# Rotary key beside the latents, norms by two blocks, and new rooms for attention's loads in a two-layer hybrid decoder

## The chip, the cores and the metric

The kernel runs on one core of a Trainium2 chip. Its time is device microseconds of one execution, as the median over runs. Engines are named as in the profile: PE (TensorE), DVE (VectorE), ACT (ScalarE), POOL (GpSimd), SP (SyncE); PEld is PE's weight load. DMA transfers are issued from the queues of SP, ACT and POOL.

## The reference

Two decoder layers of one sequence of 1024 tokens and width 1024, all in f32. In each layer:

```
h = x @ w_in                                  # split by columns into
  hg_q, hg_f, hg_i, hg_gate                   # HGRN2, 8 heads of 128: gated linear recurrence
  mla_cq (256), mla_ckv (128), mla_kr (32)    # latent attention, 8 heads
  mla_gate (512), mem_q, mem_gate             # attention into 256 memory tokens, 4 heads
q = rmsnorm(cq) @ w_uq -> 8 x (64 nope + 32 rope);  q_rope = rope(...)
c = rmsnorm(ckv);  k_nope = c @ w_uk;  v = c @ w_uv
k_rope = rope(kr)                             # one rotary key, shared by all heads
p = softmax(causal((q_nope k_nope + q_rope k_rope) / sqrt(96)));  y_mla = p v
y = concat(y_hg silu(hg_gate), y_mla silu(mla_gate), y_mem silu(mem_gate)) @ w_out
x = layernorm(4**0.25 * x + y)
```

## The kernel before

All products are made with f32 values split in two parts, a high one ("h", rounded) and a low one ("l", the rest): three matmuls for one (`mm3`, high x high, high x low, low x high). A split is an ACT cast and a DVE difference (`split`, L289 and L290; `slab_aps`, L248 and L249, for weight slabs).

A layer has five stages. (1) `mem_attn`: projections of the memory heads and attention into the memory. (2) `latents_out`: cq, ckv and kr for two halves q of the tokens, four blocks of 128 tokens each. `latents` accumulates the four blocks of a half in PSUM, over four k of the first weight slab and then over four of the second. `norm` then takes the squares of all four blocks on ACT, a power on POOL (L858) and the scaling on ACT and DVE. Once both halves are through, `turn` transposes the normalised latents on PE, scales and splits them and stores them to DRAM (CQ, CK). The raw rotary key is kept in SBUF (`kr`). `spread` loads x again, in pieces "t", and makes from the blocks of x the operands T1 to T4 of the next stage. (3) `hgrn_group`: every slab of 256 columns is projected by seven half-size products (B11, T1, T2, B22, T3, B21, T4 in this order) instead of eight, with sums before (`diff`) and after (`put`). It runs over four pairs of heads, and the last pair is followed by two slabs of gates for attention (`mla_gates`), which go through tiles "G" to DRAM (MG). (4) `mla_prep` and `mla_attend`: weights w_uv, w_uk (`kv`) and w_uq (`uq`) are loaded and split, ckT and cqT loaded back, the rotary key is made (`rope_key`, six DVE operations, three copies, eight transposes, eight splits of 64 rows into K), then keys (`k_proj`, `k_odd`), queries (`q_proj`), values (`v_proj`), scores, softmax and values. (5) `out_group`: output projection and layer norm.

The order of the instructions on every engine is written by a planner before the program runs: it takes them by their order in the code, but lets a later one go ahead if the earlier is not ready by its estimates. On the chip each engine works through its own list in order and waits at semaphores. Tiles with one tag share a fixed number of rooms (the last argument of `T`), handed out in the order in which they became free. Pools follow each other in the same bytes of SBUF, and the first write to a tile of a later pool waits until every earlier tile that overlaps any byte of it has had its last reader, a DMA store included. The rooms that matter, as byte ranges of a partition: HGRN's F 28672 to 40960 and Q 40960 to 53248, three of 4096 each; G 88384 to 96576, two; attention's weight slabs "wh" from 24576 and "wl" from 40960, two of 8192 each; the key's tile "kb" 86016 to 90112; X, the operands of the products, 163328 to 228864 (X[i][j], block row i, token half j, 16384 each); T2, T3, T4 114176 to 163328; ckT, cqT and rtab 57344 to 86016; the t pieces 82176 to 102656, over the memory values (81920 to 90112). In PSUM, HGRN's "Y" lies on the banks of the tag that the stage before took first: "A" in layer 0, "B" in layer 1.

Of the kernel before, what the change touches and what calls it, by code (L numbers as in the profile page):

```python
# [81 lines left out]
def program(tc, xT, xtok, memT, pos, w_in, small, w_uq, w_uk, w_uv, w_mk, w_mv,  # L82
# [185 lines left out]
    def xs(X, i, kc, th):  # L268
        return X[kc // 4][th][i][:, kc % 4]
# [26 lines left out]

    CQ = [[T(dr, [2, P, S], F32, f"CQd{l}{i}") for i in range(2)] for l in range(DEPTH)]
    CK = [[T(dr, [P, S], F32, f"CKd{l}{i}") for i in range(2)] for l in range(DEPTH)]
    MG = [T(dr, [4, P, S], F32, f"MGd{l}") for l in range(DEPTH)]


# [340 lines left out]
    def spread(l, X, hp, lp):  # L642

        B11, B12, B21, B22 = X[0][0], X[0][1], X[1][0], X[1][1]
        T2, T3, T4 = ([T(hp, [P, 4, 512], F32R, f"t{n}{h}", 1) for h in range(2)] for n in (2, 3, 4))

        def piece():
            return T(lp, [P, 512], F32, "t", 10)

        src = xT if l == 0 else XT1  # L650
        for k in range(4):
            raw = {}
            for i, j in ((0, 0), (0, 1), (1, 1), (1, 0)):
                raw[i, j] = piece()
                nc.scalar.dma_start(raw[i, j], src[(4 * i + k) * P:(4 * i + k + 1) * P, j * 512:(j + 1) * 512])
            t1, t2, t3, t4 = raw[0, 1], raw[1, 1], piece(), raw[1, 0]
            nc.vector.tensor_tensor(out=t3, in0=t2, in1=t1, op=ALU.subtract)
            nc.vector.tensor_tensor(out=t1, in0=t1, in1=raw[0, 0], op=ALU.subtract)
            nc.vector.tensor_tensor(out=t2, in0=t2, in1=t1, op=ALU.subtract)
            nc.vector.tensor_tensor(out=t4, in0=t4, in1=t2, op=ALU.subtract)  # L660
            for o, t in ((B12, t1), (T2, t2), (T3, t3), (T4, t4)):
                split(o[0][:, k], o[1][:, k], t)
        return dict(B11=B11, T1=B12, T2=T2, B22=B22, T3=T3, B21=B21, T4=T4)

    def hgrn_group(l, X):

        with ExitStack() as gs_:
# [93 lines left out]
                return G  # L761

            def mla_gates(i2):
                G = [T(sp, [P, S], F32, "G", 2) for _ in range(2)]
                slab_w(O_MG + 256 * i2, silu_put(G, lambda i, j, g: nc.gpsimd.dma_start(
                    MG[l][2 * i2 + i, :, j * 512:(j + 1) * 512], g)))

# [54 lines left out]
    def latents_out(l, X, tp):  # L822

        with pool(f"c{l}", bufs=1, reuse_waits="tile") as lp:
# [9 lines left out]
            def latents(q, w):  # L834
                if q == 1:
                    accs = [a[:, 512 * i:512 * i + NC] for a in (psA(), psA()) for i in range(2)]
                else:
                    accs = [psB()[:, 0:NC] for _ in range(4)]
                for half in range(2):
                    for b in range(4):  # L840
                        s_ = slice(b * P, (b + 1) * P)
                        for k in range(4):
                            kc = 4 * half + k
                            mm3(accs[b], xs(X, 0, kc, q)[:, s_], xs(X, 1, kc, q)[:, s_], w[half][0][:, k], w[half][1][:, k],
                                kc == 0, kc == KC - 1)
                return accs

            def norm(q, accs):
                cq, ck = (T(lp, [P, 4, 256], F32, "pr", 4) for _ in range(2))
                ss = T(lp, [P, 2, 4], F32, "ss", 4)  # L850
                for b in range(4):
                    for i, (c, c0, c1) in enumerate(((cq, 0, 256), (ck, 256, 384))):
                        nc.scalar.activation(c[:, b, 0:c1 - c0], accs[b][:, c0:c1], AF.Square, accum_out=ss[:, i, b:b + 1])
# [4 lines left out]
                nc.gpsimd.tensor_tensor(out=r, in0=ss.rearrange("p a b -> p (a b)"), in1=mhalf, op=ALU.pow)  # L858
                for b in range(4):
                    nc.scalar.activation(ck[:, b, 0:128], accs[b][:, 256:384], AF.Copy, scale=r[:, 4 + b:5 + b])  # L860
                    nc.vector.tensor_scalar(out=cq[:, b], in0=accs[b][:, 0:256], scalar1=r[:, b:b + 1], scalar2=None,
                                            op0=ALU.mult)
                    nc.vector.tensor_copy(kr[:, 4 * q + b], accs[b][:, 384:NC])
                return cq, ck

            def turn(si, q, cn):
                s_ = slice(q * 512, (q + 1) * 512)
                for rc in range(2 - si):
                    pt = psB()
                    for b in range(4):  # L870
                        nc.tensor.transpose(pt[:, b * P:(b + 1) * P], cn[:, b, rc * P:(rc + 1) * P], ident)
                    g = sm[:, 18 + 2 * l + rc:19 + 2 * l + rc] if si == 0 else sm[:, 22 + l:23 + l]
                    h, lo = (T(lp, [P, 512], F32R, f"c{x}", 2) for x in "hl")
                    nc.scalar.activation(h, pt, AF.Copy, scale=g)
                    nc.vector.scalar_tensor_tensor(out=lo, in0=pt, scalar=g, in1=f32(h), op0=ALU.mult, op1=ALU.subtract)
                    for i, t in enumerate((h, lo)):
                        nc.sync.dma_start(CQ[l][i][rc, :, s_] if si == 0 else CK[l][i][:, s_], f32(t))

            w = [slab_c(0), slab_c(1)]
            c1 = norm(1, latents(1, w))  # L880
            c0 = norm(0, latents(0, w))
            for q, c in ((1, c1), (0, c0)):
                for si in range(2):
                    turn(si, q, c[si])
            return spread(l, X, tp, lp)

    def mla_prep(l, lp, rp):

# [3 lines left out]
        rtab = T(lp, [P, S], F32, "rtab", 1)  # L892

        def ld_kv(raw):
            nc.sync.dma_start(raw[:, 0:512], w_uv[l])
# [33 lines left out]
        def rope_key():  # L929

            k4 = T(lp, [P, NB, P], F32, "kb", 1)
            tmp = T(lp, [P, 512], F32, "qf", 2)[:, 0:NB * RD].rearrange("p (b r) -> p b r", b=NB)
            for hv in range(2):
                a, b = (cosk, sink) if hv == 0 else (sink, cosk)
                o_ = k4[:, :, 16 * hv:16 * hv + 16]
                nc.vector.tensor_tensor(out=o_, in0=kr[:, :, 0:16], in1=a, op=ALU.mult)
                nc.vector.tensor_tensor(out=tmp, in0=kr[:, :, 16:32], in1=b, op=ALU.mult)
                nc.vector.tensor_tensor(out=o_, in0=o_, in1=tmp, op=(ALU.subtract if hv == 0 else ALU.add))
            for i in range(1, 4):
                nc.vector.tensor_copy(k4[:, :, 32 * i:32 * i + 32], k4[:, :, 0:32])  # L940
            for hf in range(2):
                pt = psB()
                for b in range(4):
                    nc.tensor.transpose(pt[:, b * P:(b + 1) * P], k4[:, 4 * hf + b], ident)
                s_ = slice(hf * 512, (hf + 1) * 512)
                split(KK[0][0][64:128, s_], KK[0][1][64:128, s_], pt[64:128])
                split(KK[1][0][0:64, s_], KK[1][1][0:64, s_], pt[0:64])

        rope_key()
        k_proj(0)  # L950
        k_odd(0)
        return cqT, ckT, KK, uq, kv, k_proj, k_odd, rtab

    def mla_attend(l, cqT, ckT, KK, uq, kv, k_proj, k_odd, rtab, lp, rp):
        uqh, uql = (t.rearrange("p (r c) -> p r c", r=2) for t in uq)
        gs = []
        qt = {}
# [19 lines left out]
                nc.gpsimd.tensor_tensor(out=ql[:, s_], in0=qf, in1=f32(qh[:, s_]), op=ALU.subtract)  # L977


        VV = T(rp, [P, NB, 8, P], F32R, "VV", 1)  # L980

        def scores(hd, j):
            kh, kl = KK[hd % 2]
# [415 lines left out]
```

## Time and profile before

| | |
|---|---|
| time, median of 3 runs | 2185.18 us (2180.64 to 2185.57) |
| profiled execution | 2189.0 us, its span 2187.2 us |
| busy: PE, PEld | 2072.6 us (95%), 1761.2 us (81%) |
| busy: DVE, ACT, POOL | 1464.6 us (67%), 1012.3 us (46%), 353.5 us (16%) |
| mean granted clock of PE | 0.980 |
| DMA | 191.32 MB, mean 87 GB/s |

An engine's row in a timeline gives the start and the length of an instruction or of a run of equal ones; in brackets stands how long the engine was idle before it, and what ended that. A granted clock of 1.00 is PE's 2.4 GHz level, 0.50 its 1.2 GHz level.

### The profile page before, as it was taken

The page shows a single profiled execution, that of the slowest core. Times are in us where ns is not written, and L with a number is a line of the kernel's source. Part 1 is how long each engine was busy: PE and PEld are TensorE (multiplying, and loading weights), DVE is VectorE, ACT ScalarE, POOL GpSimd, SP SyncE. Part 2 cuts the span into 40 slices and gives each one's busy share as a digit, 9 for nine tenths or more (in the row PEclk, how much of TensorE's full clock was granted, in tenths as well). Part 3 has the DMA queues.
Part 4 walks back from the last instruction along what each step waited for, and adds up shares of the span by engine and source line. Part 5 has one row for each costly group of instructions (what it writes and reads, how often), then busy time and mean ns, then how long its engine had stood idle before and what let it go on. Part 6 is the DMA issues. An engine that isn't in the chain of part 4 may idle for free. (4 is left out here: it accounts for less than half of the span.)

```text
span 2187.2 us, 30297 instructions
## 1 busy us (share of the span) xinstructions
PE 2072.6 (95%) x11176; PEld 1761.2 (81%) x11176; DVE 1464.6 (67%) x2665; ACT 1012.3 (46%) x2003; POOL 353.5 (16%) x480
## 2 busy tenths in 40 slices
PE   9998999999998799999999989999999987999998
PEld 7887888888887688888787878888888876888886
DVE  6536777777776688666754367777777766887424
ACT  5534343434343577544544343444343435776311
POOL 0210000000001354311111100000000013543112
PEclk9998999999999899999999989999999998999999
DMA  5314101111113301456751041011111133015322
GB/s 197 125 39 140 58 28 55 35 58 39 58 39 112 142 13 40 165 176 226 241 178 46 34 145 58 22 57 39 59 39 58 39 111 144 12 25 182 113 72 77
DMA packets 122612, 191.32 MB, mean 87 GB/s; under 512 B 8352, under 2 KB 90144, under 8 KB 122464
## 3 DMA queue, kind: packets, MB, share of 16 engines
q1 hardware_dynamic: 99408, 143.81, 20.0%
q10 hardware_dynamic: 17808, 28.54, 3.9%
q0 software_dynamic: 5248, 17.04, 2.0%
q8 instruction: 88, 1.44, 0.3%
q14 instruction: 60, 0.49, 0.1%
HBM read 148.99 MB, written 40.37 MB: 87 GB/s over the span
## 5 line engine op out<-in xcount | busy, mean ns | idle before, releaser
L263 PE MATMUL Y<-x,wh 128*128 128x512 f32 x576 | 236.7, 411 | 19.8 <-DVE G L732 10.6
L265 PE MATMUL Y<-x,wl 128*128 128x512 f32 x576 | 235.4, 409 | 1.4 <-DVE wl L290 1.4
L264 PE MATMUL Y<-x,wh 128*128 128x512 f32 x576 | 230.7, 401 | 0.0
L249 DVE TENSOR_TENSOR wl<-raw,wh 128x512 fp32r<-128x512 f32 (+2 forms) x216 | 142.0, 702 | 84.5 <-ACT wh L248 84.3
L263 PE MATMUL Y<-t,wh 128*128 128x512 f32 x432 | 171.2, 396 | 4.8 <-DVE G L732 4.8
L264 PE MATMUL Y<-t,wh 128*128 128x512 f32 x432 | 171.6, 397 | 0.0
L265 PE MATMUL Y<-t,wl 128*128 128x512 f32 x432 | 169.6, 393 | 0.0
L289 ACT CAST wh<-raw 128x512 fp32r<-128x512 f32 (+1 forms) x124 | 72.9, 592 | 203.0 <-DMA raw<-in_w_in 121.4
L248 ACT CAST wh<-raw 128x512 fp32r<-128x512 f32 (+2 forms) x216 | 118.4, 605 | 96.4 <-PE A L264 49.8
L289 ACT CAST wh<-S 128x512 fp32r<-128x512 f32 x144 | 89.2, 622 | 146.4 <-DVE S L686 63.8
L572 PEld LDWEIGHTS B<-Q,r 128*128 128x128 f32 x896 | 115.7, 191 | 38.3 <-issue 11.8
L263 PEld LDWEIGHTS Y<-x,wh 128*128 128x128 f32 x576 | 111.2, 193 | 40.3 <-DVE G L732 11.4
L1014 POOL TENSOR_SCALAR pr<-pr,rs 128x512 f32<-128x512 f32 (+1 forms) x192 | 116.8, 617 | 143.8 <-DVE rs L1011 128.8
L572 PE MATMUL B<-Q,r 128*128 128x128 f32 x896 | 132.4, 291 | 7.6 <-DVE Q L551 6.7
L290 DVE TENSOR_TENSOR wl<-raw,wh 128x512 fp32r<-128x512 f32 (+1 forms) x124 | 80.7, 656 | 85.0 <-ACT wh L289 80.7
L290 DVE TENSOR_TENSOR pl<-B,ph 128x512 fp32r<-128x512 f32 (+1 forms) x192 | 119.7, 643 | 22.2 <-ACT ph L289 19.3
L265 PEld LDWEIGHTS Y<-x,wl 128*128 128x128 f32 x576 | 110.6, 192 | 23.5 <-DVE wl L290 2.8
L264 PEld LDWEIGHTS Y<-x,wh 128*128 128x128 f32 x576 | 111.0, 193 | 20.0
L1010 ACT ACTIVATE pr<-A,nm 128x128 f32<-128x128 f32 (+7 forms) x128 | 95.6, 748 | 58.5 <-DVE nm L1007 48.9
L285 POOL TENSOR_TENSOR rst<-ss,mhalf 128x4 f32<-128x4 f32 x32 | 36.3, 1134 | 514.3 <-DVE ss L283 495.9
L289 ACT CAST ph<-B 128x512 fp32r<-128x512 f32 (+1 forms) x192 | 102.7, 553 | 31.1 <-PE B L1024 15.4
L290 DVE TENSOR_TENSOR wl<-S,wh 128x512 fp32r<-128x512 f32 x144 | 97.9, 686 | 27.3 <-ACT wh L289 26.8
(321 smaller groups left out, 5577.1 us busy)
## 6 DMA issues: line engine op xcount, KB each, us to landing
raw<-in_w_in SPq DMA_DIRECT2D x84, 512.0 KB, 4.6
raw<-in_w_out SPq DMA_DIRECT2D x32, 1024.0 KB, 5.1
yr<-Yd SPq DMA_DIRECT2D x28, 384.0 KB, 4.0
Yd<-r POOLq DMA_DIRECT2D x32, 256.0 KB, 2.6
raw<-in_w_mk SPq DMA_DIRECT2D x8, 512.0 KB, 4.5
raw<-in_w_mv SPq DMA_DIRECT2D x8, 512.0 KB, 4.6
Yd<-yt POOLq DMA_DIRECT2D x16, 256.0 KB, 2.4
t<-in_xT ACTq DMA_DIRECT2D x16, 256.0 KB, 3.3
```

The lines of the kernel that those rows point to most:

```text
L248: nc.scalar.copy(h[:, s_], raw[:, s_])
L249: nc.vector.tensor_tensor(out=lo[:, s_], in0=raw[:, s_], in1=f32(h[:, s_]), op=ALU.subtract)
L263: nc.tensor.matmul(o, lhsT=lh, rhs=rh, start=first, stop=False, **kw)
L264: nc.tensor.matmul(o, lhsT=lh, rhs=rl, start=False, stop=False, **kw)
L265: nc.tensor.matmul(o, lhsT=ll, rhs=rh, start=False, stop=last, **kw)
L285: nc.gpsimd.tensor_tensor(out=r[:, 0:k], in0=ss, in1=mhalf[:, 0:k], op=ALU.pow)
L289: nc.scalar.copy(h, src)
L290: nc.vector.tensor_tensor(out=lo, in0=src, in1=f32(h), op=ALU.subtract)
L572: nc.tensor.matmul(lp[:, pr * P:(pr + 1) * P], lhsT=xp[:, pr * P:(pr + 1) * P], rhs=q_moving(Q, pr, b), start=True, stop=True)
L1010: nc.scalar.activation(po, sv, AF.Exp, bias=nm, scale=1.0, accum_out=rs)
L1014: nc.gpsimd.tensor_scalar(out=pr[:, c0:c1], in0=pr[:, c0:c1], scalar1=rs, scalar2=0.0, op0=ALU.mult, op1=ALU.add)
```

## The change

- `mla_gates`: the gate tiles come from the rooms of F (first slab) and Q (second slab), not from G.
- `latents` and `norm` take two blocks at a time, all eight k for each; the accumulators of half 0 are three of PSUM tag B and one of A. `turn` follows its own half. Its stores, and the new ones of the rotary key, go through POOL's queue, with one tag "c" of four rooms for high and low parts.
- `rope_key` runs at the end of `latents_out`: 64 columns (the key twice), transposed, split and stored to a new DRAM tensor KR. `mla_prep` loads it from there into K, four loads on ACT's queue.
- The t pieces have nine rooms instead of ten, at the head of their pool, over the memory's transposed tokens (mT, from 57344), and are loaded through SP's queue.
- ckT, cqT and rtab move to the right-hand pool, and VV and the q tiles are placed first in it. It then spans 118272 to 228864: VV on T2 to T4, the q tiles up to 167424, ckT 167424 to 175616, cqT 175616 to 192000, K 192000 to 208384, rtab to 212480. In the left pool "kb" is at 57344, "qf" and "mg" follow, "pr" is at 82176 to 98560.

```diff
+    KR = [[T(dr, [64, S], F32, f"KRd{l}{i}") for i in range(2)] for l in range(DEPTH)]
...
-            return T(lp, [P, 512], F32, "t", 10)
+            return T(lp, [P, 512], F32, "t", 9)
...
-                nc.scalar.dma_start(raw[i, j], src[(4 * i + k) * P:(4 * i + k + 1) * P, j * 512:(j + 1) * 512])
+                nc.sync.dma_start(raw[i, j], src[(4 * i + k) * P:(4 * i + k + 1) * P, j * 512:(j + 1) * 512])
...
             def mla_gates(i2):
-                G = [T(sp, [P, S], F32, "G", 2) for _ in range(2)]
+                G = [T(hp, [P, S], F32, "FQ"[i2], 3) for _ in range(2)]
...
+            def latents(q, w, bs, accs):
+                for b in bs:
+                    s_ = slice(b * P, (b + 1) * P)
+                    for kc in range(KC):
+                        wh, wl = w[kc // 4]
+                        mm3(accs[b], xs(X, 0, kc, q)[:, s_], xs(X, 1, kc, q)[:, s_], wh[:, kc % 4], wl[:, kc % 4],
+                            kc == 0, kc == KC - 1)
...
-                    h, lo = (T(lp, [P, 512], F32R, f"c{x}", 2) for x in "hl")
+                    h, lo = (T(lp, [P, 512], F32R, "c", 4) for x in "hl")
...
-                        nc.sync.dma_start(CQ[l][i][rc, :, s_] if si == 0 else CK[l][i][:, s_], f32(t))
+                        nc.gpsimd.dma_start(CQ[l][i][rc, :, s_] if si == 0 else CK[l][i][:, s_], f32(t))
...
+            def rope_key(lp):
+                k2 = T(lp, [P, 512], F32, "t", 9).rearrange("p (b r) -> p b r", b=NB)
...
+                nc.vector.tensor_copy(k2[:, :, 32:64], k2[:, :, 0:32])
+                for hf in range(2):
+                    pt = psB()
+                    for b in range(4):
+                        nc.tensor.transpose(pt[0:64, b * P:(b + 1) * P], k2[:, 4 * hf + b], ident)
+                    h, lo = (T(lp, [P, 512], F32R, "c", 4) for x in "hl")
+                    split(h[0:64], lo[0:64], pt[0:64])
+                    for i, t in enumerate((h, lo)):
+                        nc.gpsimd.dma_start(KR[l][i][:, hf * 512:(hf + 1) * 512], f32(t)[0:64])
...
+            T(lp, [P, 512], F32, "t", 9)
             w = [slab_c(0), slab_c(1)]
-            c1 = norm(1, latents(1, w))
-            c0 = norm(0, latents(0, w))
-            for q, c in ((1, c1), (0, c0)):
+            for q in (1, 0):
+                if q == 1:
+                    accs = [a[:, 512 * i:512 * i + NC] for a in (psA(), psA()) for i in range(2)]
+                else:
+                    accs = [psB()[:, 0:NC] for _ in range(3)] + [psA()[:, 0:NC]]
+                cq, ck = T(lp, [P, 4, 256], F32, "cq", 2), T(lp, [P, 4, P], F32, "ck", 2)
+                for bs in ((0, 1), (2, 3)):
+                    latents(q, w, bs, accs)
+                    norm(q, bs, accs, cq, ck)
+                if q == 0:
+                    ops = spread(l, X, tp, lp)
                 for si in range(2):
-                    turn(si, q, c[si])
-            return spread(l, X, tp, lp)
+                    turn(si, q, (cq, ck)[si])
+            rope_key(lp)
+            return ops
...
-        ckT = [T(lp, [P, S], F32R, f"ckT{i}", 1) for i in range(2)]
-        cqT = [T(lp, [P, 2, S], F32R, f"cqT{i}", 1) for i in range(2)]
+        VV = T(rp, [P, NB, 8, P], F32R, "VV", 1)
+        for n in ("qh", "ql"):
+            T(rp, [P, S], F32R, n, 2)
+        ckT = [T(rp, [P, S], F32R, f"ckT{i}", 1) for i in range(2)]
+        cqT = [T(rp, [P, 2, S], F32R, f"cqT{i}", 1) for i in range(2)]
...
+        for i in range(2):
+            nc.scalar.dma_start(f32(KK[0][i])[64:128], KR[l][i])
+            nc.scalar.dma_start(f32(KK[1][i])[0:64], KR[l][i])
...
-        rope_key()
         k_proj(0)
```

## Rows read from the trace of the kernel before

**Rows 1.** Busy time of the engines, from the page.
```profile
PE 2072.6 (95%) x11176; PEld 1761.2 (81%) x11176; DVE 1464.6 (67%) x2665; ACT 1012.3 (46%) x2003; POOL 353.5 (16%) x480
```
**Rows 2.** PE's waits: line, releaser, us in total, times, longest.
```profile
PE B L944 <- DVE kb L940: 24.4, 2, 12.2
PE Y L263 <- DVE G L732: 15.3, 4, 5.3
PE B L871 <- ACT pr L860: 10.9, 2, 5.8
PE Y L263 <- ACT wh L289: 9.2, 2, 4.7
```
**Rows 3.** Stretches, site one: busy us by engine, clock, DMA share, GB/s.
```profile
192.90:198.70 5.80, 0.00 (x2) 0.03 (x1) 3.86 (x10) 3.46 (x11) 2.96 (x3) 0.76 0.00 0
...
208.20:213.00 4.80, 4.37 (x10) 2.97 (x11) 3.27 (x6) 1.48 (x3) 0.00 (x0) 0.50 0.50 192
```
**Rows 4.** PE's timeline at site one, layer 0: start and length in us.
```profile
192.55 0.35 PE L265 MATMUL B<-wh,x 128*128 128x416 f32 x1
198.70 4.80 PE L871 MATMUL B<-idr,pr 128*128 128x128 f32 x24 [5.80 <-ACT pr L860]
208.17 0.80 PE L263 MATMUL Y<-x,wh 128*128 128x512 f32 x1 [4.67 <-ACT wh L289]
...
212.98 0.43 PE L263 MATMUL Y<-x,wh 128*128 128x512 f32 x1
```
**Rows 5.** ACT's timeline there: the last block's squares.
```profile
194.04 0.38 ACT L853 ACTIVATE pr<-B 128x256 f32<-128x256 f32 x1
```
**Rows 6.** POOL's timeline there: the norm's power.
```profile
195.51 2.02 POOL L858 TENSOR_TENSOR rst<-ss,mhalf 128x8 f32<-128x8 f32 x1 [16.54 <-DVE ss L855]
```
**Rows 7.** A power on four columns, from the page's groups.
```profile
L285 POOL TENSOR_TENSOR rst<-ss,mhalf 128x4 f32<-128x4 f32 x32 | 36.3, 1134 | 514.3 <-DVE ss L283 495.9
```
**Rows 8.** Groups of 158 to 216 us: busy us, mean ns, idle before.
```profile
L290 DVE TENSOR_TENSOR t<-t,t 128x512 fp32r<-128x512 f32 x12 | 8.0, 685 | 3.1 <-ACT t L289 3.1
...
L874 ACT ACTIVATE ch<-B,sm 128x512 fp32r<-128x512 f32 x6 | 4.1, 687 | 4.8 <-DMA CKd<-ch 1.9 <-DMA CQd<-ch 1.6 <-PE B L871 1.3
...
L657 DVE TENSOR_TENSOR t<-t,t 128x512 f32<-128x512 f32 x4 | 2.8, 690 | 7.1 <-DMA t<-in_xT 7.1
```
**Rows 9.** DMA issues of 155 to 215 us: size, median us to landing.
```profile
CQd<-ch SPq DMA_DIRECT2D x4, 256.0 KB, 2.3
...
Yd<-yt POOLq DMA_DIRECT2D x2, 256.0 KB, 3.9
```
**Rows 10.** PE's timeline at site two, layer 0.
```profile
707.95 0.40 PE L263 MATMUL Y<-t,wh 128*128 128x512 f32 x1
...
710.49 0.39 PE L265 MATMUL Y<-t,wl 128*128 128x512 f32 x1
723.07 1.94 PE L944 MATMUL B<-idr,kb 128*128 128x128 f32 x8 [12.19 <-DVE kb L940]
...
733.43 0.30 PE L263 MATMUL A<-K,qh 128*128 128x256 f32 x1
```
**Rows 11.** Stretches of site two, columns as in rows 3.
```profile
702.70:708.00 5.30, 5.30 (x13) 4.14 (x14) 2.92 (x5) 1.71 (x3) 0.55 (x1) 0.50 0.16 63
710.90:723.10 12.20, 0.03 (x1) 0.06 (x2) 2.87 (x10) 1.21 (x2) 1.08 (x3) 0.66 0.97 384
```
**Rows 12.** DVE's timeline there: the first operation of the rotary key.
```profile
720.64 0.29 DVE L936 TENSOR_TENSOR kb<-kr,cosk 128x128 f32<-128x128 f32 x1 [7.76 <-DMA MGd<-G]
```
**Rows 13.** POOL's timeline there: the last gate store's issue.
```profile
713.18 0.54 POOL L765 DMA_DIRECT2D MGd<-G  x1 [1.68 <-DVE G L753]
```
**Rows 14.** The gate stores of both layers, from issue to landing.
```profile
DMA to landing us min/median/max: 2.3/7.8/9.6
```
**Rows 15.** SP's timeline at site two: the loads of ckT.
```profile
709.90 0.93 SPq L903 DMA_DIRECT2D ckT<-CKd  x2
```
**Rows 16.** The memory attention's stretch, columns as in rows 3.
```profile
109.40:164.00 54.60, 53.24 (x268) 44.73 (x267) 20.26 (x36) 20.69 (x49) 8.33 (x17) 1.00 0.12 39
```

More of the change, by code (lines that the diff above doesn't have):

```diff
@@ L832, in slab_c, with norm @@
                 return [t[:, 0:4 * NC].rearrange("p (k c) -> p k c", k=4) for t in slab_aps(ld, 4 * NC)]
[L834 to L851, printed above, removed]
+            def latents(q, w, bs, accs):
[5 more added lines that the diff above has]
+                            kc == 0, kc == KC - 1)
+            def norm(q, bs, accs, cq, ck):
+                n = len(bs)
+                ss = T(lp, [P, 2, 4], F32, "ss", 4)[:, :, 0:n]
+                for j, b in enumerate(bs):
                     for i, (c, c0, c1) in enumerate(((cq, 0, 256), (ck, 256, 384))):
-                        nc.scalar.activation(c[:, b, 0:c1 - c0], accs[b][:, c0:c1], AF.Square, accum_out=ss[:, i, b:b + 1])
+                        nc.scalar.activation(c[:, b, 0:c1 - c0], accs[b][:, c0:c1], AF.Square, accum_out=ss[:, i, j:j + 1])
                 for i in range(2):
@@ L857, in norm @@
                 r = T(lp, [P, 8], F32, "rst", 4)
[L858 to L861, printed above, removed]
+                nc.gpsimd.tensor_tensor(out=r[:, 0:2 * n].rearrange("p (a b) -> p a b", a=2), in0=ss,
+                                        in1=mhalf[:, 0:2 * n].rearrange("p (a b) -> p a b", a=2), op=ALU.pow)
+                for j, b in enumerate(bs):
+                    nc.scalar.activation(ck[:, b], accs[b][:, 256:384], AF.Copy, scale=r[:, n + j:n + j + 1])
+                    nc.vector.tensor_scalar(out=cq[:, b], in0=accs[b][:, 0:256], scalar1=r[:, j:j + 1], scalar2=None,
                                             op0=ALU.mult)
                     nc.vector.tensor_copy(kr[:, 4 * q + b], accs[b][:, 384:NC])
-                return cq, ck
             def turn(si, q, cn):
@@ L876, in turn @@
                     for i, t in enumerate((h, lo)):
-                        nc.sync.dma_start(CQ[l][i][rc, :, s_] if si == 0 else CK[l][i][:, s_], f32(t))
-            w = [slab_c(0), slab_c(1)]
-            c1 = norm(1, latents(1, w))
-            c0 = norm(0, latents(0, w))
-            for q, c in ((1, c1), (0, c0)):
+                        nc.gpsimd.dma_start(CQ[l][i][rc, :, s_] if si == 0 else CK[l][i][:, s_], f32(t))
+            def rope_key(lp):
+                k2 = T(lp, [P, 512], F32, "t", 9).rearrange("p (b r) -> p b r", b=NB)
+                tmp = T(lp, [P, 512], F32, "t", 9)[:, 0:NB * RD].rearrange("p (b r) -> p b r", b=NB)
+                for hv in range(2):
+                    a, b = (cosk, sink) if hv == 0 else (sink, cosk)
+                    o_ = k2[:, :, 16 * hv:16 * hv + 16]
+                    nc.vector.tensor_tensor(out=o_, in0=kr[:, :, 0:16], in1=a, op=ALU.mult)
+                    nc.vector.tensor_tensor(out=tmp, in0=kr[:, :, 16:32], in1=b, op=ALU.mult)
+                    nc.vector.tensor_tensor(out=o_, in0=o_, in1=tmp, op=(ALU.subtract if hv == 0 else ALU.add))
+                nc.vector.tensor_copy(k2[:, :, 32:64], k2[:, :, 0:32])
[7 more added lines that the diff above has]
+                        nc.gpsimd.dma_start(KR[l][i][:, hf * 512:(hf + 1) * 512], f32(t)[0:64])
@@ L891, in mla_prep @@
+        ckT = [T(rp, [P, S], F32R, f"ckT{i}", 1) for i in range(2)]
+        cqT = [T(rp, [P, 2, S], F32R, f"cqT{i}", 1) for i in range(2)]
         KK = [[T(rp, [P, S], F32R, f"K{ab}{i}", 1) for i in range(2)] for ab in range(2)]
-        rtab = T(lp, [P, S], F32, "rtab", 1)
+        rtab = T(rp, [P, S], F32, "rtab", 1)
         def ld_kv(raw):
@@ L927, in k_odd, with mla_attend @@
             nc.vector.tensor_tensor(out=KK[1][1][64:128], in0=t[64:128], in1=f32(KK[1][0][64:128]), op=ALU.subtract)
[L929 to L947, printed above, removed]
-        rope_key()
         k_proj(0)
         k_odd(0)
-        return cqT, ckT, KK, uq, kv, k_proj, k_odd, rtab
-    def mla_attend(l, cqT, ckT, KK, uq, kv, k_proj, k_odd, rtab, lp, rp):
+        return cqT, ckT, KK, uq, kv, k_proj, k_odd, rtab, VV
+    def mla_attend(l, cqT, ckT, KK, uq, kv, k_proj, k_odd, rtab, VV, lp, rp):
         uqh, uql = (t.rearrange("p (r c) -> p r c", r=2) for t in uq)
@@ L977, in q_proj @@
                 nc.gpsimd.tensor_tensor(out=ql[:, s_], in0=qf, in1=f32(qh[:, s_]), op=ALU.subtract)
-        VV = T(rp, [P, NB, 8, P], F32R, "VV", 1)
         def scores(hd, j):
```

## The prediction

> **What bounds the kernel now.** I read the page first: TensorE is busy for 2072.6 us of a span of 2187.2 [rows 1], so what a change can win lies in the 114.6 us in which it stands, and in the stretches where its clock is at half. Second, TensorE's waits by what ended them [rows 2]: three of them come twice or four times, so once or twice in each layer, and two sites hold them. Site one is the passage from the latents to the HGRN products (5.8 us for the norm's ScalarE step, 4.7 us for the first weight cast). Site two is the passage from the gate products to attention (7.6 us per layer for a gate tile, 12.2 us for the rotary key's tile). Third, the timeline of both sites in layer 0; layer 1 has the same waits, within 0.8 us.
>
> At site one the last latents matmul ends at 192.90, the 24 transposes start at 198.70, the first HGRN product at 208.17, and nine of its matmuls run before full pace is back at 212.98 [rows 4]. The granted clock falls to half in the idle stretch and is still at half (0.50, the 1.2 GHz level) up to 213 [rows 3]. A matmul of a product takes 0.23 us at full pace (eleven steps from 707.95 to 710.49 [rows 10]), so the nine are worth 2.1 us and the HGRN stage begins, in effect, at 210.9: 18.0 us after the latents. A transpose costs 0.12 us at full clock (eight in 1.94 us at half [rows 10]), so the 24 need 2.9 us and 15.1 us are lost.
>
> At site two TensorE waits 7.6 us for gate tiles, and after the second wait a product runs wholly at half clock, 5.3 us [rows 11] instead of 2.7. The last product ends at 710.88; attention's first score matmul starts at 733.43, 22.5 us later [rows 10]. The wait between them is DVE's: it stands until 720.64 for the last gate store, "MGd<-G" [rows 12], issued at 713.18 [rows 13], because the key's tile lies on the bytes of the gate tile that this store reads. So 7.5 us of store, in a stretch where the DMA engines are 0.97 busy [rows 11], sit on the path.
>
> **The change, part by part**, per layer. *Gate tiles from F and Q rooms.* Three rooms of each tag; at the last head pair at least two of each have had their last reader before the gates need them, so neither gate wait has a cause: 7.6 us, and 2.6 us of half clock, go. What is late next is only TensorE itself, so 10.2 us is taken in full (bounds: 0 if the rooms come free no earlier, 10.2).
>
> *Attention's loads.* ckT lies on X[0][0] and cqT mostly on X[0][1], operands of the last slab's first two products, so their loads can start some five products (13 us) before the projection ends; before, ckT was issued at 709.90 [rows 15]. The rotary key comes from memory (four loads of 256 KB on ScalarE's queue; two of their rooms and the rope table's lie on X[1][0], free one product before the end). I cost these loads at nothing: the key projection and q projection of head 0 (18 matmuls, 4.1 us), and the wait below, cover them. If that cover is gone, a load in a full DMA stretch costs what the gate store shows, 7.8 us [rows 14].
>
> *The wait that comes in.* Counting the rooms in the order in which the tags hand them out, MG(1)'s two tiles get the two Q rooms at bytes 40960 to 49152, and exactly these are the first "wl" slot of attention's weights, the low part of w_uv and w_uk. So DVE's four low splits (L249) wait for the same last gate store. Behind them in DVE's queue stand the key's low splits and the q products' evacuation; TensorE's low k_proj and all v_proj matmuls wait for them. What goes is the key's chain on DVE (2.4 us from 720.64 to 723.07) and its eight transposes, and TensorE can meanwhile run what needs only high parts and w_uq. Worked out from TensorE's end: store issued 2.3 us later (713.18 less 710.88), landing 4.9 us, the middle of 2.3 and 7.5 [rows 13, 14], three of the four splits 1.1, the low k_proj 0.5, cast and difference of the key 1.3, and 2.6 for one more product's length at half clock: 12.7 us against 22.5, a gain of 9.8. If the order puts k_proj's low part ahead of the q projection, that projection and its GpSimd evacuation (6.5 us) follow instead of lying beside: gain 3.3. I take 6 between the two, as the order is the planner's. Site two: 16 per layer, bounds 10 and 25 (store landed in 2.3 us, no clock loss, no wait at all for the room).
>
> One rule of the Trainium skill reads this otherwise. Rows 14 show gate stores of 256 KB landing in 2.3 to 9.6 us, median 7.8. "DMA: Bandwidth & Descriptors" (Anatomy of one DMA — SWDGE path) gives a fixed 2.0 us plus the bytes at 436 GB/s for a DMA issued by GpSimd: an estimate from it is 2.6 us. By that the sum would be 2.3 us per layer better, 2135; the trace disagrees wherever the engines are full, and I keep the trace.
>
> *Norm by two blocks.* After the last latents matmul only two blocks' chain is left. It began late (194.04 [rows 5]) and ran to 198.70; GpSimd's power takes 1.13 us on four columns [rows 7] instead of 2.02 on eight [rows 6]. I take 3.6 (bounds 2.6 and 5.8). Twelve of the 24 transposes, those of the first half, move ahead of that point and fill no gap: their 1.5 us stay.
>
> *Spread's loads on SyncE, from rooms at the memory tiles.* The t tiles leave the memory values' rooms, so loads and subtractions can start before the memory attention ends; it takes DVE 21.8 us (16 operations like L657 and 16 low splits [rows 8]) out of the way of the norm and of the weights' splits. They pass SyncE's queue, with the weight slabs behind them; 7.1 us of waits for t [rows 8] are off the path while the latents run. Cost 0.
>
> *Rotary key at the latents, stores on GpSimd's queue.* Eight transposes (1.0 us), seven DVE operations, two splits, four stores; with the turns 16 stores, 0.54 us of GpSimd each. All pairs (h, lo) go through two pairs of rooms, six before, now five after the last latents matmul. Before, a room's cycle was about 3 us (0.69 cast, issue, 2.3 landing [rows 8, 9]); with GpSimd's issue and a landing of 2.3 to 3.9 [rows 9] it is about 4. In layer 0 the first HGRN products' PSUM lies on the A rooms, free with the norm: 1.5 + 3.6 + 2.5 for the 20 transposes left and about 1 us of weights, 8.6 against 18: gain 9. In layer 1 it lies on the B rooms, which the last rope pair holds: 1.5 + 4 to the first pair, two cycles of 4, 1 for its evacuation: 14.5, gain 3.5 to 4. Site one: 13 for both layers, bounds -8 and 22.
>
> The sum is 13 + 2 x 16 = 45 us, made against the profiled execution: 2189.0 us, 2187.2 of it the span, so 2144 for that one. The median shown, 2185.18, is 0.2% below it; taking 45 from the median gives **2140**.
>
> **The rivals.** (a) *No room wait at all*, the planner handing out other rooms or the store landing at once: 22 per layer at site two and 18 in all at site one, 2185 - 62 = 2123. For it: the store lands in 2.3 us when the engines are idle. Against: my count of rooms, and about 3 MB of loads due in the same stretch.
> (b) *The room wait replaces the key's wait wholly*: only the gate waits are won, 13 + 2 x 10 = 33, 2152. For it: it is the same store, and 7.5 us is what it took last time. Against: TensorE has 18 matmuls beside it.
> (c) *Stores on GpSimd's queue land like the gate stores*, 7.8 us: the room cycle becomes some 9 us, site one turns from +13 to -8: 2161. For: rows 14; against: the engines are emptier there, and the same queue's stores took 3.9 [rows 9].
> (d) *The change doesn't do what it says*: the gates take the F room that the last head's state needs, and a wait for a room stays: 20 less, 2160. Against: head 6's room is free a whole head before.
> (e) *Slower.* The t pieces now start inside the memory attention. DVE works in order, so a subtraction that waits for its load stands before the attention's reductions and splits, and TensorE waits for those. Its whole price is 21.8 + 7.1 = 28.9 us per layer [rows 8]; it decides from 22.5 us, what both sites give per layer; at the whole price 2185 + 13 = 2198. For: DVE's order is fixed before the program runs, from estimated landings. Against: DVE works only 20.3 of 54.6 us in that stretch [rows 16].
>
> A second rule bears on (c). The trace shows 2.3 us for the SyncE stores at L877 and 3.9 for GpSimd's beside them [rows 9]. The same page (Latency and other measured facts) gives about 0.6 us to the first byte on SyncE's path and 1 us on GpSimd's: 0.4 us per store as an estimate, two room cycles, so under 1 us of layer 1's path. Its sum would be 2141, and it lends (c) nothing; only rows 14 do.
>
> **How the numbers follow.** Forecast 0.45 (its own range 2127 to 2150), (a) 0.18, (b) 0.14, (c) 0.09, (d) 0.06, (e) 0.08. The range from 2112 to 2170 leaves out (e) and the far ends of (a), (c) and (d), under 2 in 10. About 0.3%, 6.6 us, is what a measurement of this kernel can tell from no change. Slower: three quarters of (e) and a little of (c), 0.07. Same: the rest of (e) and a bad end of (c) or (d), 0.04. Faster: 0.89.
>
> **What would show it.** Right: no wait of TensorE for "G" before attention; the first wait in attention ends with L249's "wl", itself waiting for MGd<-G; first score matmul some 12 us after the last gate product, not 22.5; first HGRN product some 9 us after the latents in layer 0, later in layer 1. Wrong: TensorE waiting in the memory attention for DVE behind "t"; the rotary stores' rooms holding ScalarE for more than 5 us; a first key matmul that waits for a load.

## The result, and the profile after

The change is faster: 2159.6 us, the median of 4 runs (2158.17 to 2163.67), beside 2182.91 for the kernel before in the same session; the ratio is 0.9896, with a 95% interval of 0.9876 to 0.9917. The forecast was 2140, so about half of the 45 us came. The profiled execution went from 2189.0 to 2163.67 us, 25.3 less.

First TensorE's waits of after (line, releaser, us in total, times, longest); they answer to [rows 2].

```profile
PE B L263 <- ACT wh L248: 13.1, 2, 7.3
PE B L867 <- ACT ck L857: 12.5, 4, 4.6
PE B L889 <- DVE t L885: 7.8, 2, 3.9
PE B L573 <- DVE Q L552: 7.8, 14, 1.3
PE B L265 <- DVE wl L249: 5.7, 3, 2.7
```

The four groups of [rows 2], 59.8 us, are not there any more. But 39.1 us of others stand at the same two sites: for the norm (ck, 12.5) and the rotary key (t, 7.8) at site one, for the first weight cast and the low splits (13.1, and most of 5.7) at site two. Where the time went is read from fixed points of TensorE's timeline in both traces. "HGRN at pace" is the start of the first HGRN matmul at full pace, less 0.227 us for each matmul before it, so that a start at half clock isn't counted as a full one. Each row gives the start of a matmul; the output rows are the first and the last product of the high parts of "yh".

| start of (us) | before | after | gained since the row above |
|---|---|---|---|
| layer 0: first latents matmul | 154.75 | 153.63 | 1.1 |
| last latents matmul | 192.55 | 195.35 | -3.9 |
| HGRN at pace | 210.98 | 209.91 | 3.9 |
| last gate matmul | 710.49 | 697.59 | 11.8 |
| first score matmul | 733.43 | 716.83 | 3.7 |
| last score matmul | 896.51 | 882.16 | -2.3 |
| first output product from "yh" | 922.11 | 909.91 | -2.2 |
| last output product | 1094.33 | 1083.71 | -1.6 |
| layer 1: first latents matmul | 1248.86 | 1237.83 | 0.4 |
| last latents matmul | 1286.66 | 1281.03 | -5.4 |
| HGRN at pace | 1305.35 | 1294.34 | 5.4 |
| last gate matmul | 1806.67 | 1784.06 | 11.6 |
| first score matmul | 1829.62 | 1802.31 | 4.7 |
| last score matmul | 1992.97 | 1967.61 | -2.0 |
| last matmul | 2176.09 | 2150.74 | 0.0 |

Site one (from the first latents matmul to HGRN at pace) gives nothing in either layer. The gates' leg gives more than the 10.2 us that was forecast, and attention's start some: of 3.7 and 4.7 at the first score, 2.3 and 2.0 are given back by the last. In layer 0, 2.0 of it goes within the first head, where TensorE waits again for DVE (0.6 us for "rs", 0.5 for VV). A difference of single executions can't be trusted to some 3 us: at the transposes of layer 1's memory values TensorE waited 2.5 and 2.4 us in these two and 0.3 in that of e1 below.

Site one, TensorE's timeline of after (start and length in us, idle before and its end); the transposes answer to [rows 4].

```profile
178.17 0.33 PE L867 MATMUL B<-idr,ck 128*128 128x128 f32 x1 [2.36 <-ACT ck L857]
...
196.34 0.55 PE L867 MATMUL B<-idr,cq 128*128 128x128 f32 x3 [0.16 <-DVE cq L858]
196.72 0.38 PE L867 MATMUL B<-idr,ck 128*128 128x128 f32 x2
201.68 0.73 PE L867 MATMUL B<-idr,ck 128*128 128x128 f32 x2 [4.58 <-ACT ck L857]
202.21 1.18 PE L867 MATMUL B<-idr,cq 128*128 128x128 f32 x4
207.29 1.89 PE L889 MATMUL B<-idr,t 128*64 128x128 f32 x8 [3.91 <-DVE t L885]
208.83 0.78 PE L263 MATMUL Y<-x,wh 128*128 128x512 f32 x1
```

The stretches of after there (us, busy us of PE, PEld, DVE, ACT, POOL, granted clock, DMA share, GB/s), as in [rows 3].

```profile
195.70:201.70 6.00, 1.11 (x8) 0.69 (x7) 4.48 (x13) 3.23 (x13) 1.01 (x1) 0.92 0.00 1
203.40:207.30 3.90, 0.01 (x1) 0.04 (x2) 3.64 (x10) 2.01 (x4) 2.22 (x4) 0.50 0.39 154
207.30:211.00 3.70, 3.70 (x13) 3.06 (x14) 3.58 (x6) 2.35 (x5) 2.15 (x4) 0.51 0.75 287
```

These rows show three waits in a row on the path: 2.4 us at 178, in the middle of the second half's matmuls, for the first half's ck; 4.6 us for the last two blocks' norm; 3.9 us for the key's tile, followed by eight transposes at half clock. In layer 1 the first is as long (2.35 us), and the second is shorter:

```profile
1285.21 0.58 PE L867 MATMUL B<-idr,ck 128*128 128x128 f32 x2 [3.18 <-ACT ck L857]
```

Site two of after, TensorE's timeline; it answers to [rows 10].

```profile
697.59 0.39 PE L265 MATMUL Y<-t,wl 128*128 128x512 f32 x1
...
706.17 0.80 PE L263 MATMUL B<-ckT,wh 128*128 128x512 f32 x1 [7.31 <-ACT wh L248]
706.76 0.63 PE L264 MATMUL B<-ckT,wh 128*128 128x512 f32 x1
709.52 0.80 PE L265 MATMUL B<-ckT,wl 128*128 128x512 f32 x1 [2.14 <-DVE wl L249]
...
716.83 0.28 PE L263 MATMUL A<-K,qh 128*128 128x256 f32 x1
```

DVE's timeline, the low splits (to [rows 12]).

```profile
708.37 3.84 DVE L249 TENSOR_TENSOR wl<-raw,wh 128x256 fp32r<-128x256 f32 x8 [7.91 <-DMA MGd<-Q]
```

POOL's, the last gate store's issue (to [rows 13]).

```profile
700.76 0.54 POOL L767 DMA_DIRECT2D MGd<-Q  x1
```

ACT's queue and work there.

```profile
699.85 0.62 ACTq L935 DMA_DIRECT2D K<-KRd  x1
704.42 0.34 ACTq L939 DMA_DIRECT2D rtab<-RTd  x1
704.88 0.71 ACT L248 CAST wh<-raw 128x256 fp32r<-128x256 f32 x2 [5.61 <-DMA K<-KRd]
```

Two waits end close together. The low splits wait for the gate store, 7.6 us after its issue, as the prediction named it. And the high casts stand behind the issue of the rope table's load on ACT's queue, which waits until 704.4 for the first key load.

### The profile page after: what moved, and what is told of

Its sections match the earlier page's. It is cut to its first block, busy times and chain, and to the rows that moved or that the text cites. A ratio compares the mean times of both kernels' runs of the same rounds, so it can differ in the third digit from the quotient of the medians.

```text
span 2161.9 us, 30334 instructions
## 1 busy us (share of the span) xinstructions
PE 2065.4 (96%) x11176; PEld 1752.7 (81%) x11176; DVE 1459.8 (68%) x2665; ACT 1009.8 (47%) x1999; POOL 375.3 (17%) x516
## 5 line engine op out<-in xcount | busy, mean ns | idle before, releaser
L263 PE MATMUL Y<-x,wh 128*128 128x512 f32 x576 | 233.9, 406 | 0.0
L264 PE MATMUL Y<-x,wh 128*128 128x512 f32 x576 | 228.3, 396 | 0.0
L263 PEld LDWEIGHTS Y<-x,wh 128*128 128x128 f32 x576 | 109.6, 190 | 19.2
L263 PE MATMUL A<-wh,yh 128*128 128x512 f32 x288 | 112.7, 396 | 5.6 <-ACT wh L248 3.6
```

The lines of the kernel that those rows point to most:

```text
L263: nc.tensor.matmul(o, lhsT=lh, rhs=rh, start=first, stop=False, **kw)
L264: nc.tensor.matmul(o, lhsT=lh, rhs=rl, start=False, stop=False, **kw)
```

## The experiments

Each kernel was timed in 5 rounds beside the kernel before; the ratio is to that kernel, as for the change (0.9896), so 0.001 is 2.2 us.

**The gates' line alone.**

```diff
--- before
-                G = [T(sp, [P, S], F32, "G", 2) for _ in range(2)]
+                G = [T(hp, [P, S], F32, "FQ"[i2], 3) for _ in range(2)]
```

> The kernel before with one line of the change: attention's gate tiles G' take F and Q rooms; nothing else. Theory (the gate rooms carry nearly all of the gain): TensorE's two gate waits per layer go (the trace of after shows the last gate product 11.9 and 11.6 us earlier than its first HGRN product explains), and the rotary key no longer waits for the gate store; low weight splits wait for it instead. 23 to 32 us faster than before, 2151 to 2160, no slower than the whole change. Rival (the parts need each other: moved key, loads and rooms carry half of it): 10 to 14 us faster, 2169 to 2173.

2161.2 us, 0.9912 (0.9897 to 0.9928): one line gives 19.8 of the change's 23.3 us, and the two intervals overlap. The theory's reading holds, that this line carries nearly all of the gain; its size, 23 to 32 us, is just missed.

**All but the gates' line.**

```diff
--- after
-                G = [T(hp, [P, S], F32, "FQ"[i2], 3) for _ in range(2)]
+                G = [T(sp, [P, S], F32, "G", 2) for _ in range(2)]
```

> The whole change without the gates' line: attention's gate tiles stay in the two G rooms; all else as changed. Theory (the gate rooms carry nearly all): TensorE waits for G twice per layer again, 11.6 to 11.9 us, and what is left gives 0 to 3 us: 2178 to 2183 beside about 2181 for the kernel before. Rival (the parts overlap: with G in its old rooms the first weights' low splits no longer wait for the gate store, so attention starts earlier than in the whole change): 6 to 12 us faster than before, 2169 to 2175.

2192.95 us, 1.0056 (1.0044 to 1.0069): slower than before. Neither reading had that. TensorE's waits of this kernel:

```profile
PE Y L263 <- DVE G L733: 13.5, 4, 4.6
...
PE B L263 <- DMA ckT<-CKd: 13.0, 2, 6.8
PE B L889 <- DVE t L885: 7.8, 2, 3.9
PE B L263 <- DMA cqT<-CQd: 7.5, 2, 3.8
```

and SP's queue at site two:

```profile
693.28 14.16 SPq L1136 DMA_DIRECT2D raw<-in_w_out  x2
707.54 0.88 SPq L932 DMA_DIRECT2D ckT<-CKd  x2
708.59 8.11 SPq L938 DMA_DIRECT2D cqT<-CQd  x2
```

With the gates late, two loads of the output weights come ahead of ckT and cqT in the queue, as in the kernel before, and the second is issued 13.8 us after the first; ckT is issued at 707.54, where the whole change has it at 681.69. So the loads' cover, costed at nothing, hung on the gates' line.

**The rotary key back in attention's preparation.**

```diff
--- after
-            nc.scalar.dma_start(f32(KK[0][i])[64:128], KR[l][i])      # and K[1]
...
-            rope_key(lp)
             return ops
...
+        rope_key()            # mla_prep, as before
         k_proj(0)
```

> The whole change, but the rotary key is made in attention's preparation again (as before), not beside the latents, and isn't stored and loaded. Theory (the key beside the latents costs what the new norm and loads win at site one): the 3.9 us wait of TensorE for the key's tile t and the eight transposes at half clock (1.5 us) in front of the first HGRN product go, 4 to 5.4 us per layer; at attention the key's operations lie beside the wait for the gate store: 8 to 11 us faster than the whole change, 2149 to 2152. Rival (the key's chain returns to the path at attention: seven operations of DVE, 2.4 us, and eight transposes, 1.9 us at half clock): within 3 us of the whole change, 2157 to 2162.

2156.6 us, 0.9888 (0.9873 to 0.9903): 3 us below the change, not told apart from it, and between the two expectations. In its trace HGRN starts at 205.24 instead of 208.83, but at half clock; up to HGRN at pace site one is 1.9 us better in layer 0 and 2.8 in layer 1. The key's chain returns at site two, where TensorE waits 3.9 us for it.

**Four blocks at once.**

```diff
--- after
-                for bs in ((0, 1), (2, 3)):
-                    latents(q, w, bs, accs)
-                    norm(q, bs, accs, cq, ck)
+                latents(q, w, range(4), accs)
+                norm(q, range(4), accs, cq, ck)
```

> The whole change, with the latents normalised by all four blocks at once again (the two blocks' loop undone, the rest as changed). Theory (two blocks win a shorter tail after the last latents matmul but pay it with a wait of 2.4 us for ck inside the second half's matmuls and with the transposes there): within 3 us of the whole change, 2157 to 2163. Rival (the prediction's term, 3.6 us per layer at the tail): 7 us slower than the whole change, 2167.

2167.4 us, 0.9936 (0.9923 to 0.9948), slower than the change by more than both intervals: the rival's figure came, and the theory formed after the result falls. But it did not come at the rival's place, the tail. TensorE's timeline:

```profile
179.44 0.66 PE L867 MATMUL B<-idr,cq 128*128 128x128 f32 x2 [5.23 <-DVE kr L860]
...
205.44 1.17 PE L867 MATMUL B<-idr,cq 128*128 128x128 f32 x4 [3.71 <-DVE cq L858]
```

In the middle TensorE waits 5.2 us with four blocks, 2.4 with two, and from first to last matmul the latents take 5.5 and 3.2 us longer. After the last latents matmul it waits 3.7 us with four blocks in both layers, and 4.6 and 3.2 with two: no gain at the tail in layer 0, 0.5 us in layer 1. The rival also reads the prediction's 3.6 us as a gain; in the prediction it is the length that is left of a wait of 5.8, a gain of 2.2 per layer. So this run gives the worth of two blocks where a turn follows each half, 7.8 us, and does not bear out the term.

**The first half's turns after the second half's matmuls.**

```diff
--- after
-                if q == 0:
-                    ops = spread(l, X, tp, lp)
+                cc[q] = cq, ck
+            ops = spread(l, X, tp, lp)
+            for q in (1, 0):
                 for si in range(2):
-                    turn(si, q, (cq, ck)[si])
+                    turn(si, q, cc[q][si])
```

> The whole change, with the turns of the first half's latents written after the second half's matmuls again (as before). In the whole change TensorE, which works in order, stands 2.4 us (3.2 in layer 1) in the middle of the second half's matmuls for the first half's ck. Theory (that wait, and the twelve transposes there, 1.5 us, are what site one lost): the latents stage is 3.9 us shorter per layer, the twelve transposes lie in the 4.6 us wait for the last two blocks' norm: 5 to 8 us faster than the whole change, 2152 to 2155. Rival (all six pairs then pass two pairs of rooms after the last matmul, and a room comes back only 4 us later when its store has landed): what is won is given back at the tail, within 3 us of the whole change.

2152.6 us, 0.9871 (0.9853 to 0.9889): 7 us below the change, as the theory had it, though the intervals overlap. TensorE's timeline shows how:

```profile
192.59 1.03 PE L867 MATMUL B<-idr,cq 128*128 128x128 f32 x8
...
195.21 0.44 PE L867 MATMUL B<-idr,cq 128*128 128x128 f32 x2 [1.15 <-DVE c L871]
196.51 0.93 PE L867 MATMUL B<-idr,cq 128*128 128x128 f32 x6 [0.87 <-DVE cq L858]
...
202.48 1.89 PE L889 MATMUL B<-idr,t 128*64 128x128 f32 x8 [4.07 <-DVE t L885]
```

The wait in the middle is gone, the twelve transposes lie in the place of the 4.6 us wait, and the key's 4 us stay. The latents take 37.8 us in both layers, as in the kernel before, where the change has 41.7 and 43.2. (The 3.2 us that the expectation gives for the wait in the middle of layer 1 is the wait at its tail; in the middle it is 2.35.)

**Attention's waits at site two**, two kernels.

```diff
--- after                                          (e3_rtab_on_sync)
-        nc.scalar.dma_start(rtab, RT)
+        nc.sync.dma_start(rtab, RT)
...
-            nc.scalar.dma_start(g, MG[l][i])
+            nc.sync.dma_start(g, MG[l][i])
```

> The whole change, with the loads of the rope table and of the four gate tiles issued by SyncE in place of ScalarE. ScalarE's casts of the first attention weights stood behind the table's issue, which waited until 704.4 for the first key load. Theory A (the gate store that lands at 708.4 binds, through the low splits): TensorE's first key matmul comes at about 702, its third still at about 709.5; time within 3 us of the whole change, 2157 to 2162. Theory B (the table's issue on ScalarE's queue binds): 4 us per layer from attention's start, 2150 to 2153.

```diff
--- e3_rtab_on_sync                                (e4_rooms_rtab)
-                G = [T(hp, [P, S], F32, "FQ"[i2], 3) for _ in range(2)]
+                G = ([T(hp, [P, S], F32, "F", 3) for _ in range(2)] if i2 == 0 else
+                     [T(hp, [P, NB, P], F32, "V", 2).rearrange("p b v -> p (b v)") for _ in range(2)])
```

> As the run before it (rope table and gate tiles loaded by SyncE), and the last two gate tiles take the rooms of the HGRN values V, which are not under attention's first weights. Theory A: with the wait for the gate store gone as well, the key matmuls go through at about 702 and the first scores 6 to 8 us earlier than in the whole change: 12 to 16 us faster, 2144 to 2148. Theory B (the queue alone binds): no faster than the run before it. Theory C (the loads of the rotary key or of cqT, landing at 704 to 707, bind next): 2 to 4 us per layer, 2151 to 2156.

2164.8 (0.9925, 0.9913 to 0.9938) and 2164.4 us (0.9923, 0.991 to 0.9937): no gain, rather 5 us lost against the change by the medians, though the intervals overlap. In e3 TensorE's key matmuls come as reading A has them (the first at 700.99, the third at 708.24), but the time lies above both readings. e4 is no faster than e3, the number of its reading B, but not for the queue alone. TensorE's and SP's timelines of e4:

```profile
702.32 0.50 PE L263 MATMUL B<-ckT,wh 128*128 128x512 f32 x1 [2.81 <-ACT wh L248]
710.39 1.22 PE L263 MATMUL B<-cqT,wh 128*128 128x512 f32 x2 [6.36 <-ACT wh L248]
```

```profile
689.33 0.42 SPq L926 DMA_DIRECT2D raw<-in_w_uk  x1
702.55 0.38 SPq L929 DMA_DIRECT2D raw<-in_w_uq  x1
```

The key matmuls do run from 702.3, 2.8 us of wait for the casts in front of them, and the third no longer waits for the low splits: both waits are gone. But w_uq's load is now issued at 702.55, where the change has it at 689.15, and the query products wait for it: in the built program its issue waits for the completion semaphore that the first key load had taken, and that load landed at 702.53. In the profiled executions the largest loss is at site one of layer 1, 5.9 us in e3 and 4.4 in e4, which the edit did not touch (e3's timeline):

```profile
1287.40 1.89 PE L889 MATMUL B<-idr,t 128*64 128x128 f32 x8 [3.91 <-DVE t L885]
1292.35 0.79 PE L263 MATMUL Y<-x,wh 128*128 128x512 f32 x1 [3.06 <-DVE c L290]
```

By the addresses in the two programs the key's second transposes lie there in the PSUM bank that "Y" gets next; in the change it is another bank, and the wait is absent. This is the wait on the B rooms that the prediction put into layer 1 of the change.

**The key back, the V rooms, and the loads on SyncE together** (e2, e3 and e4 in one).

> The rotary key made in attention's preparation again, the last two gate tiles in the V rooms, the rope table and gate tiles loaded by SyncE: no key loads, no wait for the gate store, nothing but casts on ScalarE's queue. Theory (ScalarE's queue, the store and the key loads each held the first scores): TensorE's 3.3 us wait for the first weight cast after the key's transposes goes, and 2 to 3 us of half clock with it: 6 to 10 us faster than with the key moved back alone, 2147 to 2151. Rival (the load of cqT, issued at 698.4 there and 9 us long, binds the q products whatever else goes): within 3 us of that run, 2154 to 2160.

2155.2 us, 0.9876 (0.9857 to 0.9894): within 3 us of e2, the rival's figure. But cqT, the rival's cause, isn't seen in TensorE's waits; the key's transposes stand first, 3.9 us for DVE.

**The spread written after the turns**, on top of it.

```diff
--- e7_rope_rooms
-                if q == 0:
-                    ops = spread(l, X, tp, lp)
                 for si in range(2):
                     turn(si, q, (cq, ck)[si])
+                if q == 0:
+                    ops = spread(l, X, tp, lp)
```

> As the run before it, and the spread of x (its subtractions on DVE and casts on ScalarE) is written after the latents' turns, not ahead of them. Theory (ScalarE's squares of the last blocks come 1.8 us late because a cast for the spread stands before them and waits for DVE; so the norm's tail of 4.6 us shrinks to 3): 2 to 4 us faster than the run before it. Rival (the spread's later products then wait for its tiles, or the order of the norm is the same): no faster, or 2 to 4 us slower.

2152.2 us, 0.9866 (0.9853 to 0.988), not told apart from e7; the wait for the last blocks' ck is 4.58 us as before. But the order on ACT and DVE did not change there: ACT still makes a cast of the spread, which waits for DVE, ahead of the squares of the last two blocks (e8's ACT; the change has the pair at 197.01 and 197.54).

```profile
197.43 0.62 ACT L289 CAST t<-t 128x512 fp32r<-128x512 f32 x1 [0.97 <-DVE t L660]
197.96 0.38 ACT L850 ACTIVATE cq<-B 128x256 f32<-128x256 f32 x1
```

So this run does not try the spread's place, and the theory stays open.

**The key projection ahead of the rotary key**, on top of that, and then with the turns last (e9's edit) as well.

```diff
--- e8_rope_rooms_late
-        rope_key()
         k_proj(0)
+        rope_key()            # its tile in a room of pr
```

> As rope_rooms_late, and in attention's preparation the first key projection is written ahead of the rotary key, whose tile takes a room of pr. TensorE stood 3.9 us there for the key's seven to nine operations on DVE. Theory: the key matmuls run in that wait, and the first scores come 2 to 4 us earlier per layer: 4 to 8 us faster than that run, 2144 to 2148. Rival (the scores wait for GpSimd's split of the queries and for cqT, whatever comes first on TensorE): within 3 us of that run, 2149 to 2155.

> As the run before it, and the first half's turns after the second half's matmuls. If both theories hold, 10 to 14 us faster than rope_rooms_late, 2138 to 2142; if the rooms of the turns bind, no faster than the run before it.

> As the run e11_all (2142.7), but the rotary key stands ahead of the first key projection again, in its own room. Theory (the key's place is worth nothing or little there: e10 showed no gain from it): 2140 to 2146, the same as e11_all within 3 us. Rival (the order of the key matters by what its trace showed, 1.3 and 2.2 us earlier first scores per layer): 3 to 5 us slower, 2146 to 2148.

e10: 2157.9 us, 0.9889 (0.9872 to 0.9907), no faster than e8, by the medians 6 us slower with overlapping intervals; the third key matmul now waits 5.8 us for the low splits. e11: 2142.7 us, 0.9832 (0.9814 to 0.9849), the best version, 17 us below the change and clear of its interval. e12, e11 with the key in front: 2146.5 us, 0.9836 (0.9823 to 0.985), the rival's figure by the medians, but not told apart from e11 by the ratios. e12 is e8 with the turns last, and clear of it: the gain over e8 is the turns'.

## Why the prediction was half right

**The sum.** Of the 45 us forecast, 13 were put at site one and 16 per layer at site two. Site one gave nothing. Site two gave 15.5 and 16.3 us up to the first score, as forecast, but by luck: the gates gave 1.6 and 1.4 us more than was taken and attention's start 2.3 and 1.3 less. Attention then gave back 2.3 and 2.0, and the output stage of layer 0 3.7. That 2159.6 lies in the range of 2112 to 2170 is the gates' doing: their line alone, with 2161.2, lies there too.

**Gate tiles: right, in full.** 10.2 us a layer were taken, as the upper bound too; 11.8 and 11.6 came, and e1 shows that this line carries the change. Where the excess comes from stays open.

**The wait that comes in: right in kind, mis-sized.** DVE's low splits wait for the last gate store, as counted from the rooms. Of the 12.7 us from TensorE's end to the first score, the landing was put at 4.9 and took 7.6 (708.37 less 700.76), and the first score came 18.9 us after the last gate product (716.83 less 697.98), near the other order's 19.2. That order is the one on the chip: the low key product at 709.52 comes first, and the q projection and its evacuation take the 7.3 us behind it. By the last score the start is worth 1.5 and 2.8 us a layer, not 6. The rule of the Trainium skill that the prediction weighed ("DMA: Bandwidth & Descriptors", Anatomy of one DMA — SWDGE path: 2.0 us plus the bytes at 436 GB/s) gives 2.6 us as an estimate; the trace disagrees again, with the DMA engines 0.98 busy.

The stretch in which that store lands (columns as at site one):

```profile
698.85:706.20 7.35, 0.04 (x2) 0.04 (x1) 1.61 (x3) 1.62 (x5) 1.62 (x3) 0.75 0.98 315
```

**Attention's loads at nothing: wrong in two ways.** ACT's queue holds the first casts until 704.4 behind the table's issue; the landing at 708.4 hid most of it, and where e4 takes both away a third load is late in their place. And e5 shows that the loads are early only because the gates are.

**Site one: the step that failed.** "Twelve of the 24 transposes, those of the first half, move ahead of that point and fill no gap: their 1.5 us stay." They did not only stay. TensorE works in order, and they were put among the second half's matmuls before the first half's norm was done, so that TensorE waits for that norm as well, 2.4 us in each layer: the latents took 3.9 and 5.4 us longer, and e9, without that wait, has them at their old length.

The second miss is the key: eight transposes were counted (1.0 us), not that TensorE reaches them 3.9 us before DVE has made their tile, nor that they run at half clock.

The third is the norm's term in layer 0. Two blocks' chain was to end 3.6 us after the last latents matmul, with 5.8 as its bound; TensorE's wait for it ended after 6.0 us (195.70 to 201.68, with six transposes inside), no earlier than before. In layer 1 it ended after 3.8. The traces show the difference on ACT, where the last two blocks' squares stand behind a turn that waits for a room: 4.9 us in layer 0, 2.8 in layer 1. That is 2.15 us apart, and so are the two ends (5.98 and 3.83). No run takes this wait away by itself.

```profile
189.36 0.69 ACT L870 ACTIVATE c<-B,sm 128x512 fp32r<-128x512 f32 x1 [4.92 <-DMA CQd<-c]
...
1272.89 0.69 ACT L870 ACTIVATE c<-B,sm 128x512 fp32r<-128x512 f32 x1 [2.77 <-DMA CQd<-c]
```

So in layer 0 HGRN at pace came 14.2 us after the last latents matmul, where the terms left 7.1 (8.6 less the 1.5 that moved). e11, which has neither the turns in the middle nor the key, bears this out, though it holds further edits: from the first latents matmul to HGRN at pace it gains 12.6 us in layer 0 and 3.1 in layer 1, where 9 and 3.5 to 4 were forecast with the key. What limits layer 1 there is of the kind that was named, a PSUM room, held by the turns instead of the rotary key (e11's waits):

```profile
PE Y L263 <- DVE c L872: 6.6, 1, 6.6
```

**Output stage, assumed hidden: 3.7 us lost in layer 0.** The load of "yr" was issued at 903.63, at the same time as before (903.81), though attention ended 14 us earlier; TensorE stood 2.0 us for "yh". Ahead of it in SP's queue stood a load of output weights, issued at 902.97.

```profile
902.97 0.37 SPq L1136 DMA_DIRECT2D raw<-in_w_out  x1
903.63 7.60 SPq L1145 DMA_DIRECT2D yr<-Yd  x4
```

The kernel with the gates' line alone loses nothing on these legs, and in its queue "yr" goes first (e1):

```profile
889.71 10.37 SPq L1135 DMA_DIRECT2D yr<-Yd  x4
903.32 0.37 SPq L1126 DMA_DIRECT2D raw<-in_w_out  x1
```

So the loss comes with the rest of the change, and the traces point to the order in SP's queue for the wait for "yh"; what in the change sets that order was not tried.

**The signs.** No wait for "G" came. The first HGRN product starts 13.1 us after the latents in layer 0 and 11.0 in layer 1, not some 9 and later. The first wait in attention ended with the high cast, not with "wl", and the first score came after 18.9 us, not 12.

**The rivals.** (a) and (d) fell: there is a room wait, and no gate wait. The measured time lies at the prices of (c) and (d), 2161 and 2160, but not by their ways, so that is chance. At site two, 13.3 and 14.4 us a layer are left by the last score, between the forecast's 16 and (b)'s 10. (c) came in part: the stores of cq land in 5.0 us (before 2.3, [rows 9]), those of ck in 2.4, and ACT stood 6.8 us for their rooms in layer 0, 4.9 of it ahead of the last two blocks' norm. (e) did not occur; the memory attention's stretch keeps TensorE's 53.24 us of [rows 16]:

```profile
109.40:164.00 54.60, 53.24 (x269) 44.91 (x268) 20.27 (x36) 20.69 (x49) 8.33 (x17) 1.00 0.18 59
```

## What to carry to other kernels

A step moved ahead of other work on an engine that works in order brings its own producer's delay with it: ask not only what it costs but whether its input is ready at its new place. Price each part alone and each part left out; here one line was worth nearly all, and the rest without it was a loss. A room, a queue or a completion semaphore that is freed hands the wait to the next transfer of the same stretch, so look at which transfer comes next before one such wait is taken away alone.

## What the runs showed of the hardware that was not expected

An earlier start of a stage is not worth the same at full pace, because the half clock it meets can be longer or shorter: against the change, e2's first HGRN product came 3.6 us earlier after the first latents matmul in layer 0 and was worth 1.9 at pace; in layer 1 it came 2.5 us earlier and was worth 2.8. A load issued from one engine's queue can hold a load on another's, through the completion semaphore that the program gives to both: in e3 w_uq's issue moved from 689.15 to 701.34, when the first key load of ACT's queue had landed (701.32), by an edit that moved only other loads to SyncE's queue.
